# A two-layer hybrid trunk on one core: another first load of x, another order of attention's first products, a later value path in one pair

## The chip, the core and the metric

The kernel runs on one NeuronCore of a Trainium2 chip, as one program. The metric is the device time of one execution in microseconds (us), the median of the runs shown. The profile is of one such execution, taken by the hardware profiler; times in it count from the start of its span.

## The reference

Two layers over 512 tokens of width 2048, batch 1, all in float32. Cut to what matters here:

```python
for l in range(2):
    h = rms_norm(x, norm_g[l])
    proj = h @ w_in[l]                      # 2048 x 6600
    split proj into the inputs of three branches and their gates
    y_ml  = mlstm_branch(...)               # 4 heads of 128
    y_mla = mla_branch(...)                 # 8 heads, low-rank q and kv, rope, causal softmax
    y_rw, v_first = rwkv7_branch(...)       # 8 heads of 64, a recurrence over tokens
    mixed = concat(silu(z) * y for the three)
    x = x + mixed @ w_out[l]
return rms_norm(x, final_norm_g)
# in rwkv7_branch, from layer 1 on:
#   v = v + (v_first - v) * sigmoid(v0 + (v @ v1) @ v2)
# in mla_branch, per head: q from 512, k and v from 256 low-rank columns; q and k have a part with rope
```

## The kernel before

The kernel is written against a tile framework that allocates the buffers, sets the semaphores, and orders each engine's instructions by the program's order and a simulated time line; the order within an engine is then fixed. Each of the matrices is multiplied as three products of a high and a low part (`passes`: hi with xh, hi with xl, lo with xh), so each operand is split first: ScalarE rounds it to the high part (line 150 for weights, 252 for features), VectorE, or GpSimd for attention's weights, subtracts (lines 151, 254, 256).

*The start.* `load_x` reads x, 512 x 2048, in 16 pieces of 256 KB as four tiles `xb` with tokens on the partitions. TensorE transposes them (`feature_major`, line 301), 4 transposes for each of 16 feature tiles, and the result is scaled by `ngc`, the norm's gain, while it is split into `xh` and `xl`. ScalarE sums the squares of the 16 pieces (line 280) for the norm's factor `rb`, which `rstd_cols` spreads by the products `psrs` (line 291). `rb` is applied only to the finished gemm (`normed`, line 542), so the gemm can run before it is known.

*The gemms.* `w_in` is taken in blocks of 256 columns (`ORDER`: `rk0`, `misc`, `rr0`, ... in layer 0), each in four weight tiles `raw` of 512 KB, of which two fit (`Stream`, `wload`, `wsplit`). One block is 96 products of 128 x 512. A block is a generator of eight steps in `bg`; other work calls `bg.step()` or `bg.ensure(name)` and so places the steps in the program. Weights come through SyncE's queue, `nc.sync.dma_start`, with nearly all other loads and stores.

*PSUM.* Eight banks: tag a (`bank`, two), b (`bank2`, two), g (`gbank`, three, for the gemms and attention's up-projections), h (`bank3`, one).

*The recurrence.* `rw_pair(p)` makes the triangular inverse of two heads for eight chunks of 64 tokens, from 16 x 16 blocks up to 32 (`psQ`, `psT`) and 64 (`psQ` again, `psX`), and applies it to two right sides in `AR` (`psW`): one from keys, one, `psR` (line 928), from the values `UV`. In layer 1 the values need gemms `rv0` and `rv1` (line 891) and `psv`, line 893. Each yield lets one gemm step in.

*Attention.* `heads_order` gives the order of generators: `head_in` (products `psqn` and `pskn` of one head), `pair_rope` (`psqr` of two heads and `rope`, VectorE instructions in lines 1234 to 1237), `pair_v` (`psv`, two banks), `head_scores` and `head_out`. The weights are streamed in the same order. While it begins, VectorE also has the end of the gemms (`sg_az`) and the splits `ml` of mixed features left to do.

Of the kernel before, what the change touches and what calls it, by code (L numbers as in the profile page):

```python
# [30 lines left out]
def heads_order():  # L31

    yield from (("rope", 0), ("in", 0), ("v", 0))
    for h in range(8):
        if h < 7:
            yield "in", h + 1
        yield "scores", h
        if h % 2 == 1 and h < 7:
            yield "rope", h // 2 + 1
        yield "out", h  # L40
        if h % 2 == 1 and h < 7:
            yield "v", h // 2 + 1
# [31 lines left out]
def trunk(ctx, tc, a, out):  # L74
# [37 lines left out]
    ngr = x0p.tile([32, 128], F32, name="ngr")  # L112
    dma(ngr, a["norm_g"].rearrange("l (r c) -> (l r) c", c=128))
    xb0 = [x0p.tile([128, D], F32, tag=f"xb{tb}", name=f"xb{tb}_0") for tb in range(4)]

    def load_x(q):

        for tb in range(4):
            dma(xb0[tb][:, q * 512:q * 512 + 512], a["x"][0, tb * 128:(tb + 1) * 128, q * 512:q * 512 + 512])
    load_x(0)  # L120


# [9 lines left out]
    act(warm, eps_rms, AF.Sqrt)  # L132

# [87 lines left out]
    def gemm(l, name, finish, tmajor=False):  # L221

        def run():
            ps = [gbank(f"pg{u}_{name}{l}") for u in range(2)]
# [151 lines left out]
    ngc = const.tile([128, 32], F32, name="ngc")  # L376
    nc.vector.tensor_copy(ngc, ps[:, 0:32])
    onec = ones[:, 0:1][:, :, None]
    ss = sum_squares(x0p, "x0")
# [137 lines left out]
    for l in range(DEPTH):  # L517
# [117 lines left out]
        if l == 0:  # L635
            x_tiles(0)
            for q in range(4):
# [56 lines left out]
        def rw_pair(p, l=l):  # L694
# [194 lines left out]
            v = fetch("rv")  # L889
            if l > 0:  # L890
                bg.ensure("rv1")
                ps = bank(f"psv2_{nm}")
                mm(ps, lhsT=v2[:, p * 128:(p + 1) * 128], rhs=kept["vv"], start=True, stop=True)
                yield
                s = tmp("vs")
                sigm(s, ps, pch(R_V0 + p))
                vf = tmp("vf")
                dma(vf, vf_d[p])
                tt(vf, vf, v, ALU.subtract)
                tt(vf, vf, s, ALU.mult)  # L900
                tt(v, v, vf, ALU.add)
            tt(bv, bv, v, ALU.mult)
            dma(tail_d[p, 0], bv)

            UV = rp.tile([128, 2, 8, 64], F32, tag="UV", name=f"UV{nm}")
            token_major(lambda tb: v[:, tb * 128:(tb + 1) * 128], lambda h: UV[hs[1 - h], h], "v")
# [26 lines left out]
            nc.scalar.copy(AR[:, even, 64:128], psR[0])  # L933
            nc.scalar.copy(AR[hs[0], odd, 64:128], psR[1][hs[1]])
            nc.vector.tensor_copy(AR[hs[1], odd, 64:128], psR[1][hs[0]])
# [17 lines left out]
            for j in (1, 3):  # L953
                nc.scalar.copy(Q[q4[j], odd, :], psQ[1][q4[j ^ 2]])
                nc.vector.tensor_copy(Q[q4[j], even, :], psQ[0][q4[j]])
            yield
            with in_order():
                psX = cross32([(3, 2), (1, 0)], lambda i, c: Q[q4[i], c, :], lambda i, c: X32[q4[i], c, :], "psX64",
                              (bank, bank2), (0, 1))
            for j in (0, 2):  # L960
                nc.scalar.copy(X[q4[j], odd, 32:64], psX[1][q4[j ^ 2]])
                nc.vector.tensor_copy(X[q4[j], even, 32:64], psX[0][q4[j]])
            yield
# [570 lines left out]
_INS = ['x', 'positions', 'norm_g', 'w_in', 'ml_conv_w', 'ml_conv_b', 'ml_i_bias', 'ml_f_bias', 'ml_norm_g',  # L1534
# [21 lines left out]
```

## Time and profile before

| | |
|---|---|
| median of 3 runs | 1965.5 us (1965.09 to 1966.24) |
| the profiled execution | 1964.04 us, its span 1962.3 us |
| TensorE busy | 1932.2 us, 98% |
| VectorE, ScalarE, GpSimd busy | 1245.6, 863.5, 136.4 us |
| mean granted clock of TensorE | 0.997 of full speed |
| read from and written to HBM | 212.45 and 50.35 MB |

The span runs from the first to the last instruction. A busy TensorE is one with a matmul in flight: matmuls are pipelined and overlap, so the sum of their durations is more than the time they take one after the other. The granted clock tells which share of full speed (2.4 GHz) the chip gave TensorE in a stretch; half of it is the lower level, 1.2 GHz.

### The profile page before, as it was taken

To read this page: it belongs to the slowest core of one execution; us is meant where nothing else is said; L and a number is where in the kernel's file an instruction comes from. 1 tells how busy PE (TensorE), PEld (TensorE's weight loads), DVE (VectorE), ACT (ScalarE), POOL (GpSimd) and SP (SyncE) were. 2 spreads that over 40 slices of the span, in tenths; PEclk is the share of its full clock that TensorE was granted. 3 is DMA by queue.
4 is the path that set the end of the run, shared out by engine and by line. 5 is a ranking of instruction groups with operands and counts; after the bars stand their busy time and mean duration, and the time that the engine had idled before them with its cause. 6 is when DMAs were issued, how large, how long until landed. Compare 5 with 4: busy or idle time off the path is not lost. (4 is left out here: it accounts for less than half of the span.)

```text
span 1962.3 us, 31796 instructions
## 1 busy us (share of the span) xinstructions
PE 1932.2 (98%) x12544; PEld 1607.1 (82%) x12544; DVE 1245.6 (63%) x2179; ACT 863.5 (44%) x1509; POOL 136.4 (7%) x168
## 2 busy tenths in 40 slices
PE   8999999999999999999999999999999999999998
PEld 6888888888888878788888788988878888788886
DVE  6876776685766398533366558676847676884343
ACT  6534352434556356422263234433434564563233
POOL 4010010100000031000001001010100000210000
PEclk9999999999999999999999999999999999999999
DMA  5443444335655443334444444344345564343334
GB/s 178 131 141 106 126 127 119 115 110 173 188 167 177 120 119 121 103 136 133 135 111 138 121 122 129 118 131 122 106 125 189 167 209 137 105 133 115 118 121 158
DMA packets 246394, 264.86 MB, mean 135 GB/s; under 512 B 49972, under 2 KB 178174, under 8 KB 246246
## 3 DMA queue, kind: packets, MB, share of 16 engines
q1 hardware_dynamic: 245398, 261.88, 43.8%
q8 instruction: 98, 1.61, 0.3%
q0 software_dynamic: 848, 0.97, 0.2%
q14 instruction: 50, 0.41, 0.1%
HBM read 212.45 MB, written 50.35 MB: 134 GB/s over the span
## 5 line engine op out<-in xcount | busy, mean ns | idle before, releaser
L1405 PE MATMUL po<-whi_o,mh 128*128 128x512 f32 x512 | 200.2, 391 | 0.1
L1405 PE MATMUL po<-whi_o,ml 128*128 128x512 f32 x512 | 199.3, 389 | 0.0
L151 DVE TENSOR_TENSOR wlo_o<-raw_o,whi_o 128x1024 fp32r<-128x1024 f32 x64 | 78.3, 1225 | 188.7 <-ACT whi_o L150 187.6
L1405 PE MATMUL po<-wlo_o,mh 128*128 128x512 f32 x512 | 187.8, 390 | 0.0
L150 ACT ACTIVATE whi_o<-raw_o 128x1024 fp32r<-128x1024 f32 x64 | 67.7, 1059 | 204.7 <-PE po L1405 168.2
L1405 PEld LDWEIGHTS po<-whi_o,mh 128*128 128x128 f32 x512 | 96.1, 188 | 20.1 <-DVE Vl L254 0.6
L1405 PEld LDWEIGHTS po<-wlo_o,mh 128*128 128x128 f32 x512 | 96.0, 188 | 20.0
L1405 PEld LDWEIGHTS po<-whi_o,ml 128*128 128x128 f32 x512 | 96.2, 188 | 19.7
L239 PE MATMUL pg_az<-xl,whi_az 128*128 128x512 f32 x256 | 100.7, 393 | 0.0
L239 PE MATMUL pg_az<-xh,whi_az 128*128 128x512 f32 x256 | 100.6, 393 | 0.0
L239 PE MATMUL pg_az<-xh,wlo_az 128*128 128x512 f32 x256 | 99.5, 394 | 0.0
L235 PE MATMUL pg_mv<-whi_mv,xh 128*128 128x256 f32 x256 | 72.9, 285 | 0.0
L235 PE MATMUL pg_mv<-whi_mv,xl 128*128 128x256 f32 x256 | 72.7, 285 | 0.0
L235 PE MATMUL pg_mv<-wlo_mv,xh 128*128 128x256 f32 x256 | 72.4, 285 | 0.0
L770 POOL TENSOR_TENSOR bk<-kk,Ei 64x512 f32<-64x512 f32 x16 | 26.5, 1657 | 505.2 <-DVE kk L757 176.5
L151 DVE TENSOR_TENSOR wlo_az<-raw_az,whi_az 128x1024 fp32r<-128x1024 f32 x32 | 39.1, 1223 | 31.0 <-ACT whi_az L150 30.8
L239 PEld LDWEIGHTS pg_az<-xh,wlo_az 128*128 128x128 f32 x256 | 48.1, 188 | 9.5
L239 PEld LDWEIGHTS pg_az<-xh,whi_az 128*128 128x128 f32 x256 | 48.1, 188 | 9.4
L239 PEld LDWEIGHTS pg_az<-xl,whi_az 128*128 128x128 f32 x256 | 48.2, 188 | 9.3
L239 PE MATMUL pg_rk<-xh,whi_rk 128*128 128x512 f32 x128 | 50.9, 401 | 1.3 <-ACT xh L252 1.3
L239 PE MATMUL pg_rk<-xl,whi_rk 128*128 128x512 f32 x128 | 51.5, 403 | 0.0
L150 ACT ACTIVATE whi_az<-raw_az 128x1024 fp32r<-128x1024 f32 x32 | 33.7, 1053 | 39.7 <-PE pg_az L239 26.6
(576 smaller groups left out, 5547.7 us busy)
## 6 DMA issues: line engine op xcount, KB each, us to landing
raw_o<-in_w_out_dram SPq DMA_DIRECT2D x64, 512.0 KB
raw_az<-in_w_in_dram SPq DMA_DIRECT2D x32, 512.0 KB
raw_rk<-in_w_in_dram SPq DMA_DIRECT2D x16, 512.0 KB
raw_rr<-in_w_in_dram SPq DMA_DIRECT2D x16, 512.0 KB
raw_rv<-in_w_in_dram SPq DMA_DIRECT2D x16, 512.0 KB
raw_rz<-in_w_in_dram SPq DMA_DIRECT2D x16, 512.0 KB
raw_mq<-in_w_in_dram SPq DMA_DIRECT2D x16, 512.0 KB
raw_mk<-in_w_in_dram SPq DMA_DIRECT2D x16, 512.0 KB
```

Source lines behind the costliest of these rows:

```text
L150: act(hi, raw, AF.Copy)
L151: (nc.gpsimd if name[0] == "u" or name in ("misc0_0", "misc0_1") else nc.vector).tensor_tensor(lo, raw, hi.bitcast(F32), ALU.subtract)
L235: mm(ps[u][:, (tb % 2) * 256:(tb % 2) * 256 + 256], lhsT=xx[:, sl], rhs=w[:, i, :], start=(k == 0 and n == 0 and tb % 2 == 0), stop=(k == ...
L239: mm(ps[u], lhsT=w[:, i, u * 128:(u + 1) * 128], rhs=xx, start=(k == 0 and n == 0), stop=(k == 15 and n == 2))
L770: nc.gpsimd.tensor_tensor(bk[q, :, slot, :], x[q].rearrange(c64, t=64), Ei[q].rearrange(c64, t=64), ALU.mult)
L1405: mm(pss[tb], lhsT=xx[:, sl], rhs=w, start=(k == korder[0] and j == 0), stop=(k == korder[15] and j == 2))
```

## The change

*The start.* The host passes x transposed (`xt`) and the gains transposed (`norm_gt`) as further inputs. The first weight tile is loaded first, then `ngc` directly, then 16 feature tiles `xr` of 256 KB, which are split without a transpose. After them x is loaded once more with tokens on the partitions, in four loads of 1 MB, for four squares. Fourteen products of zeros run on TensorE at the beginning. The `misc` gemm of layer 0 takes banks of tag a instead of g.

*Attention.* The first three entries of the order become in, rope, v.

*Layer 1, pair 0.* Fetching the values, their residual, the transposes to `UV` (now the inner function `values`) and `psR` with its three copies move behind the inverse's second level: `values` ahead of the products `psX`, and `psR` right behind these, in banks a and b.

```diff
-    yield from (("rope", 0), ("in", 0), ("v", 0))
+    yield from (("in", 0), ("rope", 0), ("v", 0))
...
-    ngr = x0p.tile([32, 128], F32, name="ngr")
-    dma(ngr, a["norm_g"].rearrange("l (r c) -> (l r) c", c=128))
-    xb0 = [x0p.tile([128, D], F32, tag=f"xb{tb}", name=f"xb{tb}_0") for tb in range(4)]
+    xr = [x0p.tile([128, T], F32, tag=f"xr{k}", name=f"xr{k}") for k in range(16)]
     def load_x(q):
-        for tb in range(4):
-            dma(xb0[tb][:, q * 512:q * 512 + 512], a["x"][0, tb * 128:(tb + 1) * 128, q * 512:q * 512 + 512])
-    load_x(0)
+        for k in range(4 * q, 4 * q + 4):
+            dma(xr[k], a["xt"][k * 128:(k + 1) * 128, :])
...
+    zero = x0p.tile([128, T], BF16, name="zero")
+    nc.vector.memset(zero, 0.0)
+    ps = bank2("pswarm")
+    for _ in range(14):
+        mm(ps, lhsT=zero[:, 0:128], rhs=zero, start=True, stop=True)
...
-            ps = [gbank(f"pg{u}_{name}{l}") for u in range(2)]
+            ps = [(bank if (l, name) == (0, "misc") else gbank)(f"pg{u}_{name}{l}") for u in range(2)]
...
     ws.ahead(raws=1)
-    load_x(1)
+    ngc = const.tile([128, 32], F32, name="ngc")
+    dma(ngc, a["norm_gt"])
+    load_x(0)
     ws.ahead()
-    load_x(2)
-    load_x(3)
-    ps = bank("psng")
-    nc.tensor.transpose(ps[:, 0:32], ngr, idf[0:32, 0:32])
...
+    for q in range(1, 4):
+        load_x(q)
+    ss = sum_squares(x0p, "x0")
+    xb0 = [x0p.tile([128, D], F32, name=f"xb{tb}_0") for tb in range(4)]
+    for tb in range(4):
+        dma(xb0[tb], a["x"][0, tb * 128:(tb + 1) * 128, :])
...
-                    feature_major(0, k, lambda tb: xb0[tb][:, k * 128:k * 128 + 128], (bank, bank2)[k % 2])
+                    split2(xh[k], xl[k], xr[k], scale=ngc[:, k:k + 1])
...
-            for q in range(4):
-                for tb in range(4):
-                    add_square(x0p, ss[:, tb, q:q + 1], xb0[tb][:, q * 512:q * 512 + 512], f"x0_{tb}_{q}")
+            for tb in range(4):
+                add_square(x0p, ss[:, tb, 0:1], xb0[tb], f"x0_{tb}")
...
+            late = l > 0 and p == 0
...
+            if not late:
+                for _ in values():
+                    yield
...
-                psR = cross(64, lambda h, c: GG[hs[1 - h], h, c, 0:64], lambda h, c: UV[hs[1 - h], h, c, :], "psR",
-                            (bank2, bank2))
+                if not late:
+                    psR = right((bank2, bank2))
...
+            if late:
+                for _ in values():
+                    yield
             yield
             with in_order():
                 psX = cross32([(3, 2), (1, 0)], lambda i, c: Q[q4[i], c, :], lambda i, c: X32[q4[i], c, :], "psX64",
                               (bank, bank2), (0, 1))
+                if late:
+                    psR = right((bank, bank2))
...
+            if late:
+                right_back(psR)
             yield
```

## Rows read from the trace of the kernel before

**Rows 1.** The page's table of engines: busy us, share of the span, instructions.
```profile
PE 1932.2 (98%) x12544; PEld 1607.1 (82%) x12544; DVE 1245.6 (63%) x2179; ACT 863.5 (44%) x1509; POOL 136.4 (7%) x168
```
**Rows 2.** The waits of TensorE: us in total, times, the longest.
```profile
PE psv L1291 <- DVE qrf L1236: 5.0, 2, 2.6
...
PE psTv L779 <- DVE TX L862: 0.6, 1, 0.6
```
**Rows 3.** Stretches of the start: length, busy per engine, granted clock, DMA share, GB/s.
```profile
2.00:10.00 8.00, 4.26 (x17) 3.11 (x17) 2.23 (x11) 4.43 (x12) 6.09 (x17) 1.00 0.88 267
10.00:18.00 8.00, 7.16 (x30) 5.58 (x31) 5.13 (x7) 6.88 (x15) 4.83 (x17) 0.79 1.06 391
12.20:15.60 3.40, 3.40 (x11) 2.48 (x10) 1.75 (x4) 2.30 (x6) 3.04 (x14) 0.51 1.07 398
20.00:24.00 4.00, 4.00 (x23) 3.29 (x22) 2.24 (x7) 3.97 (x10) 0.00 (x0) 1.00 0.04 10
43.40:100.00 56.60, 56.60 (x254) 46.31 (x253) 46.84 (x63) 30.59 (x37) 4.79 (x5) 1.00 0.47 134
```
**Rows 4.** Timeline of SyncE's queue from 7 us on, and ScalarE's last split of `rk0`.
```profile
7.33 6.85 SPq L119 DMA_DIRECT2D xb<-in_x_dram  x8
14.79 0.38 SPq L323 DMA_DIRECT2D raw_rk<-in_w_in_dram  x1
...
23.34 0.40 SPq L323 DMA_DIRECT2D raw_rk<-in_w_in_dram  x1
...
27.12 1.06 ACT L150 ACTIVATE whi_rk<-raw_rk 128x1024 fp32r<-128x1024 f32 x1 [1.43 <-DMA raw_rk<-in_w_in_dram]
```
**Rows 5.** Timeline of TensorE: the first gemm's first products, the second gemm's first.
```profile
11.23 0.47 PE L239 MATMUL pg_rk<-xh,whi_rk 128*128 128x512 f32 x1
11.54 0.39 PE L239 MATMUL pg_rk<-xl,whi_rk 128*128 128x512 f32 x1
11.77 0.40 PE L239 MATMUL pg_rk<-xh,whi_rk 128*128 128x512 f32 x1
...
43.42 0.40 PE L239 MATMUL pg_misc<-xh,whi_misc 128*128 128x512 f32 x1
```
**Rows 6.** Groups by line, 0 to 45 us: busy us, mean ns, idle before.
```profile
L301 PE MATMUL psx<-idf,xb 128*128 128x128 f32 x64 | 11.9, 318 | 3.5 <-DMA xb<-in_x_dram 3.3
L280 ACT ACTIVATE junk_x<-xb 128x512 f32<-128x512 f32 x16 | 10.0, 625 | 3.0 <-DMA xb<-in_x_dram 2.9
L150 ACT ACTIVATE whi_rk<-raw_rk 128x1024 fp32r<-128x1024 f32 x4 | 4.2, 1054 | 2.1 <-DMA raw_rk<-in_w_in_dram 2.1
L132 ACT ACT_TABLE_LOAD x1 | 1.3, 1283 | 0.8 <-PEq L1544 0.8
L291 PE MATMUL psrs<-idf,sg_rw 128*128 128x128 f32 x8 | 1.1, 274 | 0.0
```
**Rows 7.** Stretches where attention begins, layers 0 and 1, and layer 1's pair 0.
```profile
688.00:698.00 10.00, 7.42 (x35) 5.90 (x34) 9.91 (x12) 4.80 (x9) 3.35 (x2) 1.00 0.67 214
698.00:702.00 4.00, 4.00 (x23) 4.00 (x23) 4.00 (x6) 3.10 (x6) 1.82 (x1) 0.57 0.63 193
1673.00:1680.00 7.00, 6.91 (x45) 6.14 (x44) 6.91 (x10) 4.71 (x8) 1.87 (x1) 1.00 0.39 109
1040.00:1180.00 140.00, 140.00 (x945) 110.31 (x944) 80.20 (x118) 47.45 (x69) 7.43 (x5) 1.00 0.41 123
```
**Rows 8.** Timeline of attention's beginning: layer 0, then layer 1.
```profile
694.00 0.68 DVE L1234 TENSOR_TENSOR rt<-psqr,sinn 32x512 f32<-32x512 f32 x1
698.84 1.82 POOL L151 TENSOR_TENSOR wlo_uqk<-raw_uqk,whi_uqk 128x768 fp32r<-128x768 f32 x1 [5.42 <-ACT whi_uqk L150]
702.31 0.40 PE L1263 MATMUL psqn<-cqh,whi_uqk 128*128 128x512 f32 x1
...
1669.02 0.68 DVE L1234 TENSOR_TENSOR rt<-psqr,sinn 32x512 f32<-32x512 f32 x1
1676.19 0.40 PE L1263 MATMUL psqn<-cqh,whi_uqk 128*128 128x512 f32 x1
```

More of the change, by code (lines that the diff above doesn't have):

```diff
@@ L369, in trunk @@
     ws.ahead(raws=1)
-    load_x(1)
+    ngc = const.tile([128, 32], F32, name="ngc")
+    dma(ngc, a["norm_gt"])
+    load_x(0)
     ws.ahead()
-    load_x(2)
-    load_x(3)
-    ps = bank("psng")
-    nc.tensor.transpose(ps[:, 0:32], ngr, idf[0:32, 0:32])
-    ngc = const.tile([128, 32], F32, name="ngc")
-    nc.vector.tensor_copy(ngc, ps[:, 0:32])
+    for q in range(1, 4):
[4 more added lines that the diff above has]
+        dma(xb0[tb], a["x"][0, tb * 128:(tb + 1) * 128, :])
     onec = ones[:, 0:1][:, :, None]
-    ss = sum_squares(x0p, "x0")
     prm, prh, omu, gbias = [], [], [], []
@@ L636, in trunk @@
             x_tiles(0)
+            xh, xl = xT[0]
             for q in range(4):
                 for k in range(4 * q, 4 * q + 4):
-                    feature_major(0, k, lambda tb: xb0[tb][:, k * 128:k * 128 + 128], (bank, bank2)[k % 2])
+                    split2(xh[k], xl[k], xr[k], scale=ngc[:, k:k + 1])
                 if q == 1:
@@ L888, in rw_pair, with values, right, right_back @@
             yield
[L889 to L903, printed above, removed]
-            UV = rp.tile([128, 2, 8, 64], F32, tag="UV", name=f"UV{nm}")
-            token_major(lambda tb: v[:, tb * 128:(tb + 1) * 128], lambda h: UV[hs[1 - h], h], "v")
+            late = l > 0 and p == 0
+            UV = rp.tile([128, 2, 8, 64], F32, tag="UV", name=f"UV{nm}")
+            def values():
+                v = fetch("rv")
+                if l > 0:
+                    bg.ensure("rv1")
+                    ps = bank(f"psv2_{nm}")
+                    mm(ps, lhsT=v2[:, p * 128:(p + 1) * 128], rhs=kept["vv"], start=True, stop=True)
+                    yield
+                    s = tmp("vs")
+                    sigm(s, ps, pch(R_V0 + p))
+                    vf = tmp("vf")
+                    dma(vf, vf_d[p])
+                    tt(vf, vf, v, ALU.subtract)
+                    tt(vf, vf, s, ALU.mult)
+                    tt(v, v, vf, ALU.add)
+                tt(bv, bv, v, ALU.mult)
+                dma(tail_d[p, 0], bv)
+                token_major(lambda tb: v[:, tb * 128:(tb + 1) * 128], lambda h: UV[hs[1 - h], h], "v")
+            def right(banks_):
+                return cross(64, lambda h, c: GG[hs[1 - h], h, c, 0:64], lambda h, c: UV[hs[1 - h], h, c, :], "psR", banks_)
+            def right_back(psR):
+                nc.scalar.copy(AR[:, even, 64:128], psR[0])
+                nc.scalar.copy(AR[hs[0], odd, 64:128], psR[1][hs[1]])
+                nc.vector.tensor_copy(AR[hs[1], odd, 64:128], psR[1][hs[0]])
+            if not late:
+                for _ in values():
+                    yield
             for _ in range(2):
@@ L932, in rw_pair @@
             tt(Q[:, even, :], psQ[0], mqb, ALU.mult)
-            nc.scalar.copy(AR[:, even, 64:128], psR[0])
-            nc.scalar.copy(AR[hs[0], odd, 64:128], psR[1][hs[1]])
-            nc.vector.tensor_copy(AR[hs[1], odd, 64:128], psR[1][hs[0]])
+            if not late:
+                right_back(psR)
             yield
@@ L955, in rw_pair @@
                 nc.vector.tensor_copy(Q[q4[j], even, :], psQ[0][q4[j]])
+            if late:
+                for _ in values():
+                    yield
             yield
@@ L962, in rw_pair @@
                 nc.vector.tensor_copy(X[q4[j], even, 32:64], psX[0][q4[j]])
+            if late:
+                right_back(psR)
             yield
@@ L1530, in trunk @@
     x_ctx.close()
-_INS = ['x', 'positions', 'norm_g', 'w_in', 'ml_conv_w', 'ml_conv_b', 'ml_i_bias', 'ml_f_bias', 'ml_norm_g',
+_INS = ['x', 'positions', 'xt', 'norm_gt', 'w_in', 'ml_conv_w', 'ml_conv_b', 'ml_i_bias', 'ml_f_bias', 'ml_norm_g',
         'mla_q_norm_g', 'mla_w_uq', 'mla_kv_norm_g', 'mla_w_ukv', 'rw_mu', 'rw_w0', 'rw_w2', 'rw_a0', 'rw_a2',
@@ L1545 @@
     arrays, args = {}, {}
+    inputs["xt"] = np.asarray(inputs["x"])[0].T
+    inputs["norm_gt"] = np.asarray(inputs["norm_g"]).reshape(-1, 128).T
     for name in _INS:
```

## The prediction

> **What bounds the kernel now.** I read the page's table of engines first: TensorE is busy for 1932.2 of 1962.3 us [rows 1]. Work taken off another engine gains nothing by itself; the change can win or lose only where TensorE waits, runs at the lower clock, or does work that can go, and all its idle time together is 30.1 us. The view of TensorE's waits says where that idle time lies as far as it has a releaser: above all two waits of products `psv` for VectorE, 5.0 us in all, the longer 2.6 [rows 2]. Most of the rest is the start and the end. At the start the first real product begins at 11.23, and the second gemm (`misc`) at 43.42 [rows 5]. From 43.4 to 100 us TensorE is busy for 56.60 of 56.60 [rows 3], so 43.42 is the mark against which the start is measured: what moves it moves the end.
>
> **The change at the start.** It has two sides.
>
> What goes: 64 transposes `psx`, 11.9 us of overlapped busy time [rows 6]. The first gemm has 96 products 0.23 us apart [rows 5], 21.9 us of work, and took 32.2 us from 11.23 to 43.42. If data were there, TensorE could begin at about 7 us (half a MB of weights and a quarter MB of x at 267 GB/s from 2 us on [rows 3], the landing, the splits) and be through at about 31.
>
> What comes: x is loaded a second time, by four loads of 1 MB, and in the program these stand behind the features and ahead of the third weight tile, which can't be asked for before the first one is split, since there are two raw buffers. SyncE issues in the order of the program: in the trace the last pieces of x, then the third weight tile at 14.79, then 15 small parameter loads, then the fourth at 23.34 [rows 4]. All go into one queue. Up to the third tile it held 16 x 0.262 + 3 x 0.524 = 5.77 MB. From 2 to 18 us, 267 x 8 + 391 x 8 = 5.26 MB came; the last 0.51 at 391 GB/s end at 19.3, and from 20 us on the rate is 10 [rows 3]: the tile landed last in line. With 4.19 MB more in front of it, at 391, it lands 10.7 us later, at 30.0. A page of the Trainium skill, "DMA: Bandwidth & Descriptors" (section Measured), has 425 GB/s for its largest transfer. By that figure the extra x takes an estimated 9.9 us and the sum is 0.8 us less; no transfer here has rows as long as the new loads'.
>
> TensorE then does 48 of the 96 products early, by about 19, and stands until the third tile is split. ScalarE does that in 1.05 us [rows 6]. In the program the squares of the four x blocks come ahead of it. A square of 512 columns takes 0.625 us and a copy of 1024 takes 1.054 [rows 6], so a square of 2048 is about 1.9, and 2.1 with the read-out of its sum, an estimate from these two. The last block lands 1.3 us before the weights (0.524 MB at 391), at 28.7, is squared by 30.8, and the split ends at 31.9. With the split first it is 31.1; with the norm's square root and its table load (1.3 [rows 6], and 0.4 for the rest, an estimate) ahead as well, 33.6. I take 31.9, since both earlier things are ready earlier.
>
> From there: 48 products at 0.23 are 10.9 us. The clock: after the sparse start 3.4 us had a granted clock of 0.51, the 1.2 GHz level [rows 3]; that costs 3.4 x 0.5 = 1.7 us. I take it again after a hole of some 12 us, although the 14 warming products have been run: these help only the 48 products that must wait anyhow. The granted clock was also 0.57 from 698 to 702, behind a wait of 2.6 us, and 1.00 from 1673 to 1680, behind one of 2.4 [rows 2, 7]; this hole is longer than both. The Trainium skill's page "TensorE: Matmul & The Clock Gate" (section HAM oscillation) has an array that waits for DMA fall back to half rate, which speaks against warming it ahead of such a wait. By that rule the sum stays; were the clock kept, it is 1.7 us less.
>
> The 8 products `psrs` (1.1 us as busy time [rows 6]), the parameters' transposes and one small one stay, about 1.2 us together, behind the hole, as what they need lands late too. Sum: 31.9 + 10.9 + 1.7 + 1.2 = 45.7 against 43.42: **+2.3 us**. Bounds: 31.1 + 10.9 + 1.2 = 43.2, so -0.2; and 33.6 + 13.8 = 47.4, so +4.0. The fourth tile is what is late next: issued at about 14.79 + 10.7 + 8.55 = 34.0, split from 3.8 us after its issue (27.12 against 23.34 [rows 4]), so by 38.9, and wanted at 31.9 + 5.5 + 1.7 = 39.1. It is just covered; each us more costs one.
>
> The other edits here cost nothing on that path: `ngc` comes by a 16 KB load instead of a transpose, `misc` takes PSUM banks that nobody else asks for before it ends, and four squares stand for 16.
>
> **Attention's first products.** Before, the order is rope, in, v. There are three gemm banks, so the first `psv` takes the bank of `psqr`, which VectorE empties by five rope instructions of 0.68 us. They begin at 694.0, at the end of a backlog (VectorE is busy for 9.91 of 10 us), so TensorE stands 2.6 us and then runs at 0.57 [rows 2, 7, 8]. Layer 1 has the same with 2.4 us. After, `psv` takes the bank of `psqn`, which is free after one ScalarE and one VectorE instruction. I leave VectorE's backlog as it is: from 694.0 it then does the low parts of q and k (1.4) and then the rope (3.4). `psv` can start at 694.7, before TensorE arrives at 695.1 (702.31 less its own products, the slow clock and the wait). Its 24 products of half width (2.8) end at 697.9; now the next head's `psqn` takes the bank of `psqr`, free at 698.8, and wants low weights that GpSimd had ready at 700.7 [rows 8]. It began at 702.31 before, so 1.6 to 3.5 us are won. In layer 1: 1669.0 + 1.4 + 3.4 = 1673.8 against 1676.19 [rows 8], 2.4 us. Part is given back, for VectorE has no room (4.00 of 4.00 us [rows 7]) and the first scores wait for its rope parts. I take 1.5 per layer, about half of what the rows would allow: **-3.0 us**. Bounds: both waits and the slow stretch whole (2.6 + 2.4 + 4 x 0.43 = 6.7), -6.7; and 0, if the wait only moves to the next `psqn` or the scores.
>
> **Layer 1's first right sides.** The inverse of pair 0 no longer waits for gemm rv1. From 1040 to 1180 us, where that pair lies, TensorE is busy for 140.00 of 140 us [rows 7]: the wait is filled with gemm, and the same products come in another order. The 32 products `psR` and the three copies behind them move ahead of `psW`; the gemm that is left covers them, and without it they are about a microsecond. Cost 0. What it shifts is where the later pairs fall against the gemms, bounded by a wait such as that of `psTv`, 0.6 [rows 2], either way.
>
> **Sum.** The profiled execution took 1964.0 (span 1962.3). 1964.0 + 2.3 - 3.0 + 0 = 1963.3; the median shown is 1.5 above that execution, so **1964.8**. About 0.2% (3.9 us) is what a measurement of this kernel can tell from no change; this is inside it.
>
> **The rivals.**
> 1. The start pays in full: the third weight tile is issued ahead of the second copy of x. For it: x comes 4 us sooner and 64 transposes are gone. Against: the loads kept the program's order up to here [rows 4]. Then `misc` begins at 7 + 21.9 + 1.2 + 1 = 31, 12.3 sooner: 1964.8 - 2.3 - 12.3 = 1950.2.
> 2. Slower: the second copy runs at 267 GB/s, the rate of the first 8 us, instead of 391. Then 4.19 MB take 15.7, all behind the hole is 5.0 later, and the time is 1969.8. It decides against the change (+3.9) below 270 GB/s or so. For it: nothing shows the rate of such loads; against: from 10 us on it was up and stayed.
> 3. The hole is as long, but the split goes first and the clock holds (-0.2), and attention gives 5: 1965.5 - 5.2 = 1960.3.
> 4. Attention does not do what it says, the wait moves whole: 1967.8, inside my own case.
>
> **Chances.** The forecast, with 1961.6 to 1969.4 as its own range, 0.46; rival 1 0.18; rival 2 and what else makes the start late 0.17; rival 3 0.19, of which a little falls short of 0.2%. So faster by over 0.2% 0.35, within 0.2% 0.48, slower 0.17. The range 1951 to 1970.5 holds the forecast, rival 3, half of rival 1 and most of rival 2.
>
> **What would show it.** TensorE idle for about 12 us between 19 and 32, released by ScalarE's split of the third `rk` tile; half clock behind it; `misc` beginning near 46. At 690 to 705 no wait of `psv` for the rope, but one of a microsecond before the next `psqn`. Nothing idle at layer 1's first pair, before or after. The prediction is wrong if the third tile is issued ahead of the four large loads, if these take much less or more than 10.7 us, or if TensorE stands elsewhere for what has been moved.

## The result, and the profile after

The changed kernel takes 1976.61 us (median of 4 runs, 1976.29 to 1977.52) against 1965.87 (1965.09 to 1967.93) for the kernel before, measured beside it: a ratio of 1.0056 [1.0043, 1.0068]. It is slower by about 10.7 us, and outside the predicted range. The profiled execution took 1976.29, its span is 1974.6, 12.3 us more than that of before.

The page's table of engines of the changed kernel, which answers to [rows 1]:

```profile
PE 1930.9 (98%) x12493; PEld 1603.2 (81%) x12493; DVE 1240.1 (63%) x2179; ACT 860.1 (44%) x1485; POOL 139.7 (7%) x168
```

TensorE is busy 1.3 us less than before and idle 13.6 us more. Its waits, by line and releaser (us in total, times, longest), say where, as [rows 2] did:

```profile
PE ps_prm L410 <- DMA gbias<-in_ml_f_bias_dram: 15.0, 1, 15.0
PE psqn L1290 <- DVE qrf L1263: 5.0, 2, 4.1
PE psv L1318 <- DVE qrf L1263: 2.1, 2, 1.1
...
PE psT L940 <- issue: 1.2, 1, 1.2
...
PE pg_rk L243 <- DVE wlo_rk L155: 0.9, 1, 0.9
```

The first is one hole of 15 us, and its releaser is not the third weight tile but small loads behind it. The profile puts it down to the last of them, `gbias`; by the program the transposes need the thirteen that go to `pt`. The second is where the wait for the rope has gone, which the new attention order was to shrink: before it stood at `psv` [rows 2]. TensorE's time line at the start (start, duration, line, tile, count, idle before and releaser), to be read against [rows 5]:

```profile
18.05 0.39 PE L243 MATMUL pg_rk<-xh,wlo_rk 128*128 128x512 f32 x1
33.48 0.89 PE L410 MATMUL ps_prm<-idf,pt 128*128 128x128 f32 x2 [15.04 <-DMA gbias<-in_ml_f_bias_dram]
34.02 0.77 PE L243 MATMUL pg_rk<-xh,whi_rk 128*128 128x512 f32 x1
...
36.94 0.80 PE L243 MATMUL pg_rk<-xh,wlo_rk 128*128 128x512 f32 x1 [0.86 <-DVE wlo_rk L155]
...
40.94 0.86 PE L243 MATMUL pg_rk<-xh,wlo_rk 128*128 128x512 f32 x2
41.65 0.40 PE L243 MATMUL pg_rk<-xh,whi_rk 128*128 128x512 f32 x1
...
43.73 0.39 PE L243 MATMUL pg_rk<-xh,whi_rk 128*128 128x512 f32 x1
43.96 1.05 PE L295 MATMUL psrs<-idf,sg_rw 128*128 128x128 f32 x8
```

After 48 products TensorE stands from 18.4 to 33.5. The two transposes of the parameters come next in its order, ahead of the third tile's products. Behind them products start 0.43 us apart up to 41.65 and 0.23 after: half clock for nearly 8 us. The products of the fourth weight tile begin at 43.73. SyncE's time line, against [rows 4], shows what they waited for:

```profile
13.43 2.43 SPq L384 DMA_DIRECT2D xb<-in_x_dram  x4
16.39 0.38 SPq L327 DMA_DIRECT2D raw_rk<-in_w_in_dram  x1
17.19 0.34 SPq L404 DMA_DIRECT2D pt<-in_ml_conv_b_dram  x1
...
18.34 0.25 SPq L404 DMA_DIRECT2D pt<-in_mla_q_norm_g_dram  x1
20.76 0.23 SPq L404 DMA_DIRECT2D pt<-in_mla_kv_norm_g_dram  x1
23.23 0.31 SPq L404 DMA_DIRECT2D pt<-in_rw_mu_dram  x1
25.63 0.25 SPq L404 DMA_DIRECT2D pt<-in_rw_w_dram  x1
28.08 0.25 SPq L404 DMA_DIRECT2D pt<-in_rw_a_dram  x1
...
31.01 0.31 SPq L407 DMA_DIRECT2D pt<-in_rw_r_k_dram  x1
...
32.11 0.40 SPq L327 DMA_DIRECT2D raw_rk<-in_w_in_dram  x1
```

From 18.3 to 28.1 a small load goes out only every 2.4 us, and each such moment is one at which a block of `xb` lands: ScalarE's squares wait for the four blocks and begin at 20.83, 23.29, 25.70 and 28.14. Two of them, and the splits of the third and the fourth weight tile, in ScalarE's time line:

```profile
20.83 1.91 ACT L284 ACTIVATE junk_x<-xb 128x2048 f32<-128x2048 f32 x1 [1.68 <-DMA xb<-in_x_dram]
23.29 1.91 ACT L284 ACTIVATE junk_x<-xb 128x2048 f32<-128x2048 f32 x1 [0.47 <-DMA xb<-in_x_dram]
...
30.05 1.04 ACT L154 ACTIVATE whi_rk<-raw_rk 128x1024 fp32r<-128x1024 f32 x1
...
37.03 1.06 ACT L154 ACTIVATE whi_rk<-raw_rk 128x1024 fp32r<-128x1024 f32 x1 [5.75 <-DMA raw_rk<-in_w_in_dram]
```

The third tile was split from 30.05 on. TensorE could not use it before 33.5, because an instruction ahead in its queue wanted something else. VectorE's time line shows the same there:

```profile
33.97 0.29 DVE L412 COPY prm<-ps_prm 128x128 f32<-128x128 f32 x1 [3.60 <-PE ps_prm L410]
...
35.70 1.18 DVE L155 TENSOR_TENSOR wlo_rk<-raw_rk,whi_rk 128x1024 fp32r<-128x1024 f32 x1
...
38.12 1.23 DVE L155 TENSOR_TENSOR wlo_rk<-raw_rk,whi_rk 128x1024 fp32r<-128x1024 f32 x1 [1.15 <-ACT whi_rk L154]
```

The copies of the parameters out of `ps_prm` stand ahead of the low part of the third tile, which so is made only at 35.70; that is the 0.86 us for which TensorE waits once more, at 36.94. The fourth tile, last in SyncE's order, went out at 32.11; both its parts were there at 39.4, over 4 us before its first product.

How the delay runs on: first starts of some tiles (of the two in layer 1 the last start), in us, from the line of each tile in the trace, with the two parts alone (s1: the start alone, s2: the attention order alone).

| start of | before | after | s1 | s2 |
|---|---|---|---|---|
| gemm `misc`, layer 0 | 43.4 | 50.4 | 50.5 | 43.7 |
| gemm `rz` | 115.3 | 122.3 | 122.4 | 115.7 |
| gemm `mq` | 217.1 | 225.6 | 227.6 | 217.5 |
| gemm `az` | 588.3 | 597.3 | 599.8 | 588.4 |
| `po`, layer 0 | 791.8 | 800.0 | 803.6 | 791.5 |
| last `az`, layer 1 | 1661.6 | 1671.0 | 1674.7 | 1661.2 |
| last `po`, layer 1 | 1953.1 | 1965.8 | 1967.5 | 1956.8 |

Of 12.7 us at the end, 7.0 are lost before `misc`, 1.5 between `rz` and `mq`, and 3.3 in layer 1's attention; in layer 0's attention 0.8 are won.

### The profile page after: what moved, and what is told of

The parts are those of the page before. It is cut to its first block, busy times and chain, and to the rows that moved or that the text cites. A ratio compares the mean times of both kernels' runs of the same rounds, so it can differ in the third digit from the quotient of the medians.

```text
span 1974.6 us, 31684 instructions
## 1 busy us (share of the span) xinstructions
PE 1930.9 (98%) x12493; PEld 1603.2 (81%) x12493; DVE 1240.1 (63%) x2179; ACT 860.1 (44%) x1485; POOL 139.7 (7%) x168
## 5 line engine op out<-in xcount | busy, mean ns | idle before, releaser
L155 POOL TENSOR_TENSOR wlo_uqk<-raw_uqk,whi_uqk 128x768 fp32r<-128x768 f32 x16 | 29.7, 1858 | 593.9 <-ACT whi_uqk L154 590.7
```

Source lines behind the costliest of these rows:

```text
L155: (nc.gpsimd if name[0] == "u" or name in ("misc0_0", "misc0_1") else nc.vector).tensor_tensor(lo, raw, hi.bitcast(F32), ALU.subtract)
```

## The experiments

Each ratio is to the kernel before, run beside it. s4 to s7, s9, s15 and s16 are edits of the changed kernel, so they also have its attention order, which alone costs 2.3 us (s2).

### The parts alone: s1, s2, s3

**s1_start** is before with the start of the change alone, all of it (the features, the second load, the zeros, the banks for `misc`). Its core:

```
-                    feature_major(0, k, lambda tb: xb0[tb][:, k * 128:k * 128 + 128], (bank, bank2)[k % 2])
+                    split2(xh[k], xl[k], xr[k], scale=ngc[:, k:k + 1])
...
+    for tb in range(4):
+        dma(xb0[tb], a["x"][0, tb * 128:(tb + 1) * 128, :])
```

> The kernel before with the start alone changed (features first, second copy of x, warming products, other banks for misc). Theory 1: nearly all of the start's loss is TensorE standing before the two parameter transposes, which it meets ahead of the third weight tile's products and whose small loads are queued behind the 4 MB of x; so the same hole of about 15 us from 18.4 to 33.5, half clock until about 41.6, misc beginning near 50.4 instead of 43.4, and +7.0 to +8.5 us in all: 1973 to 1974.5 against 1965.9. Rival (the prediction's own step, the hole ends with the third tile, and what is worse in the changed kernel comes from the mixture of edits): misc near 46, about 1968.

1976.67 us, 1.0054 [1.0041, 1.0067]. The start alone costs as much as the whole change: the wait at `ps_prm` is 15.2 us and `misc` begins at 50.5.

**s2_order** is before with the order alone:

```
-    yield from (("rope", 0), ("in", 0), ("v", 0))
+    yield from (("in", 0), ("rope", 0), ("v", 0))
```

> The kernel before with the new order of attention's first products alone. Theory 1: the wait for the rope goes over to the next psqn and in layer 1 grows to about 4 us, since VectorE has two splits of mixed rows ahead of the rope in its order, and these wait for loads that wait for a buffer; layer 0 gains about 1, layer 1 loses about 3: +2 us, 1968 (1966.5 to 1969). Rival (the prediction's term): -3, 1963.

1967.95 us, 1.0014 [1.0006, 1.0023]: a loss of 1.2 to 4.5 us in place of the predicted gain. TensorE's waits, and VectorE's time line where layer 1's attention begins:

```profile
PE psqn L1263 <- DVE qrf L1236: 4.7, 2, 3.8
```

```profile
1667.39 0.67 DVE L254 TENSOR_TENSOR ml<-mr,mh 128x512 fp32r<-128x512 f32 x1
...
1671.23 1.34 DVE L254 TENSOR_TENSOR ml<-mr,mh 128x512 fp32r<-128x512 f32 x2 [2.55 <-ACT mh L252]
1672.59 0.68 DVE L1234 TENSOR_TENSOR rt<-psqr,sinn 32x512 f32<-32x512 f32 x1
```

Two splits of mixed rows stand ahead of the rope in VectorE's order. Their row was asked for at 1668.10, when the split at 1667.39 had given back one of three buffers `mr`; it landed at 1670.57, ScalarE's part came behind it, and VectorE stood for 2.55 us with the rope's operand ready. TensorE's next `psqn`, and windows behind it (stretch, its length and busy time of PE, PEld, DVE, ACT, POOL with counts, granted clock, DMA share, GB/s):

```profile
1676.22 0.77 PE L1263 MATMUL psqn<-cqh,whi_uqk 128*128 128x512 f32 x1 [3.78 <-DVE qrf L1236]
```

```profile
1676.00:1680.00 4.00, 3.78 (x9) 3.04 (x10) 4.00 (x5) 0.81 (x2) 1.70 (x1) 0.50 0.45 115
1680.00:1684.00 4.00, 4.00 (x14) 3.14 (x14) 2.11 (x4) 2.05 (x5) 0.00 (x0) 0.71 0.01 2
```

So this `psqn` begins when it did before (1676.19 [rows 8]): what the order had won is gone. The loss comes behind it: a granted clock of 0.50 and 0.71 in place of 1.00 is 3.2 us of work in these 8, and the next `psv` waits 1.07 us for the second rope.

**s3_late** is before with the late right sides alone, as in the change's diff:

```
+            late = l > 0 and p == 0
...
-                psR = cross(64, lambda h, c: GG[hs[1 - h], h, c, 0:64], lambda h, c: UV[hs[1 - h], h, c, :], "psR",
-                            (bank2, bank2))
+                if not late:
+                    psR = right((bank2, bank2))
...
+                if late:
+                    psR = right((bank, bank2))
```

> The kernel before with layer 1's first right sides made with the last product of the inverse, alone. Theory 1: TensorE has gemm to do either way, so 0 to +1.2 us, 1966 to 1967. Rival (the prediction's term): exactly nothing, 1965.9 within 0.6; a gain of more than 1 us would speak against both.

1965.52 us, 0.9996 [0.9988, 1.0005]: nothing.

### What in the start costs: s4, s5, s6, s7, s9, s15, s16

**s4_defer** asks for the second copy only behind the fourth weight tile:

```
-    for tb in range(4):
-        dma(xb0[tb], a["x"][0, tb * 128:(tb + 1) * 128, :])
...
+            for tb in range(4):
+                dma(xb0[tb], a["x"][0, tb * 128:(tb + 1) * 128, :])
```

> The changed kernel, with the four 1 MB loads of x issued behind the fourth weight tile instead of ahead of the third. Theory 1: the third tile is early and the hole shrinks, but the parameters' loads are still issued only from about 14 us on, and TensorE meets their transposes at about 17; it stands some 5 us there, until 22 or so; misc begins at 36 to 38, 12 to 14 us sooner than in the changed kernel: 1963 to 1965. Rival (the hole belongs to the third weight tile alone): no stand at all before misc, which begins near 31; 19 us sooner, 1957.

1974.15 us, 1.0041 [1.0028, 1.0055]. The hole shrank (`ps_prm` waits 4.2 us) and `misc` began at 40.1, but now the 4.19 MB lie ahead of the weights of `misc`, whose products stood twice for ScalarE's part, 3.1 us together, once for GpSimd's low part (1.8) and once for VectorE's (0.8), and the norm was late. So 10.3 us won at `misc` are 2.5 in the time. The transfer costs ahead of the third tile, and also behind the fourth.

**s5_nocopy** has no second copy and squares the 16 feature tiles instead. Its sums run over the tokens, not over the features, so it doesn't compute the norm; it only shows what the copy costs:

```
-    for tb in range(4):
-        dma(xb0[tb], a["x"][0, tb * 128:(tb + 1) * 128, :])
...
-            for tb in range(4):
-                add_square(x0p, ss[:, tb, 0:1], xb0[tb], f"x0_{tb}")
+            for k in range(16):
+                add_square(x0p, ss[:, k % 4, k // 4:k // 4 + 1], xr[k], f"x0_{k}")
```

> The changed kernel without the second copy of x; the squares for the norm are taken from the feature tiles instead, so the norm's sums are other sums (16 squares of 512 columns). Theory 1 (the 4 MB are what is too much, in two places: ahead of the third tile and the parameters, and, once moved, ahead of the misc weights): TensorE still stands some 4 us before the parameter transposes, until about 22.5, but finds the misc weights there; misc begins at 36 to 38 and runs without a stop: 1962 to 1964. Rival (the misc weights are late by themselves, by their small pieces and GpSimd's splits): the stops of 6 us inside misc stay, 1969.

1968.74 us, 1.0012 [1.0003, 1.0021], 7.9 below the changed kernel. `misc` begins at 40.2 and does not stop; `ps_prm` still waits 3.6 us, and 2.6 us go at the third tile's low part, which VectorE again makes behind the copies out of `ps_prm`. So the copy is the larger part, and the small loads cost also without it. The time is the rival's, but by another way: the lead of 3.2 us at `misc` is 0.8 at layer 0's `az`, and from layer 1's `az` to its last weight tile of `po`, with the changed kernel's attention order, 3.4 are lost.

**s6_packed** keeps the copy where it was and packs the parameters on the host, one load and one for the gate biases per layer:

```
-                for r, s in srcs:
-                    n = s.shape[0] // 128
-                    pdma(pt[r:r + n, :], s.rearrange("(r c) -> r c", c=128))
...
+                pdma(pt, a["prm"][l])
```

> The changed kernel with each layer's parameters packed on the host into one 128 x 128 array, so that one load and one for the gate biases stand where 15 stood; x's second copy stays where it is. Theory 1 (SyncE gets a new load out only as an older one lands, so the 15 small loads take until 32 and hold both the transposes and the fourth tile): the hole ends with the third tile at about 31.5 instead of 33.5, no wait for the fourth tile; misc near 47.5: 1973.5. Rival (the small loads cost nothing beside the 4 MB): 1976.6, as the changed kernel.

1971.16 us, 1.0026 [1.0015, 1.0037], 5.4 below the changed kernel, where 3.1 were expected: 13 small loads fewer. `ps_prm` begins at 29.18 after 10.4 us, the third tile's products at 30.67, `misc` at 45.1.

**s7_pieces** packs them too, and loads the copy in 16 pieces of 256 KB behind the fourth tile, into the buffers of the features.

```
+                for q in range(4):
+                    xb = x0p.tile([128, T], F32, tag=f"xr{4 * tb + q}", name=f"xb{tb}_{q}")
+                    dma(xb, a["x"][0, tb * 128:(tb + 1) * 128, q * 512:q * 512 + 512])
+                    add_square(x0p, ss[:, tb, q:q + 1], xb, f"x0_{tb}_{q}")
```

> The packed parameters, and x's second copy in 16 pieces of 256 KB that are loaded into the buffers of the features, behind the fourth weight tile, with 16 squares. Theory 1: both causes gone; TensorE stands 2 to 4 us around 17 to 21 for the third tile (5.8 MB have to come first at some 390 GB/s), misc begins at 32 to 34, without stops: about 17 us sooner than the changed kernel, 1959 (1957 to 1962). Rival (something else in the start is slow, or the misc weights are late again): 1965 or more.

1967.85 us, 1.0014 [1.0005, 1.0023]. `misc` begins at 36.2, but TensorE stands 7.7 us about it: for the weights of `misc` (3.2 for ScalarE's part, 2.2 for GpSimd's) and for the norm (`psrs`, 2.3). The lead at the mark is given back behind it.

**s9_prmlate** was meant to put the transposes behind the third tile's products, but left TensorE's order as it was, since at that point of the program only 36 of the 96 products stand ahead of them; in the trace they still come behind the 48th.

```
-                nc.tensor.transpose(ps[:, 0:128], pt, idf)
+                tc.keep_in_program_order(nc.tensor.transpose(ps[:, 0:128], pt, idf))
```

> The changed kernel with the two parameter transposes pinned behind the third weight tile's products in TensorE's order; all loads stand where they were. Theory 1 (the transposes wait for the last of 15 small loads, 2.4 us after the third tile is there): the hole ends when the third tile is split, at 31.1 instead of 33.5, but the fourth tile, whose load is still issued at about 32 behind the small ones, is now waited for by about 3 us; so no more than 0 to 2 us are won: 1974.5 to 1976.6. Rival (the place of the transposes is the whole difference between prediction and result): as the packed parameters, 1971.

1976.46 us, 1.0054 [1.0041, 1.0068], `ps_prm` waits 14.8 and `misc` begins at 50.6: it says nothing on the place of the transposes. But its fourth tile went out at 31.12, ahead of the two loads of the gate biases, so the place of these two loads changes nothing.

**s16_prmlate2** does it: three more steps of the gemm come first in the program, and the transposes are issued behind the last of these products, the 72nd. The two loads of the gate biases come later with them, so that the fourth tile goes out ahead of these two, as in s9.

```
-                nc.tensor.transpose(ps[:, 0:128], pt, idf)
+                third = next(i for i in reversed(nc.cur_bb.bb.instructions) if i.engine == mybir.EngineType.PE)
+                with tc.issue_after(third):
+                    nc.tensor.transpose(ps[:, 0:128], pt, idf)
...
+            for _ in range(3):
+                bg.step()
```

> The changed kernel with the two parameter transposes really behind the third tile's products in TensorE's order (three more steps of the gemm are traced ahead of them); the loads stand as they were. Theory 1 (small loads late, and the fourth tile's load behind them): the hole ends at 31.1 with the third tile, 2.4 us sooner, and the wait for the fourth tile grows; 1974 to 1976. Rival (only the place of the transposes was wrong in the prediction): as the packed parameters, 1971.

1973.28 us, 1.0044 [1.0029, 1.0060], 3.3 below the changed kernel; its profiled span is 5.2 shorter. TensorE's time line and windows:

```profile
30.72 0.80 PE L243 MATMUL pg_rk<-xh,whi_rk 128*128 128x512 f32 x1 [12.36 <-ACT whi_rk L154]
...
35.58 0.45 PE L243 MATMUL pg_rk<-xh,whi_rk 128*128 128x512 f32 x1
```

```profile
34.00:36.00 2.00, 2.00 (x7) 1.57 (x6) 0.00 (x0) 0.87 (x1) 0.00 (x0) 0.58 0.99 289
36.00:38.00 2.00, 2.00 (x11) 1.61 (x10) 1.78 (x3) 0.19 (x1) 0.49 (x2) 1.00 0.57 75
```

The hole is now released by the split, as the prediction had it: 12.4 us, half clock until 35.6, no wait for a low part, the fourth tile in time as in the changed kernel, `misc` at 45.6. In this execution the loads ran some 0.4 us earlier, which is part of the 4.8 won at `misc`. The time falls between the two theories and its interval holds both, so the step is read from the trace and not from the time.

**s15_nowarm** is the changed kernel without its 14 products of zeros.

```
-    for _ in range(14):
-        mm(ps, lhsT=zero[:, 0:128], rhs=zero, start=True, stop=True)
```

> The changed kernel without the 14 warming products. Theory 1 and the prediction alike: the first 48 products wait for the third tile anyhow, so nothing: 1976.6 within 1. Rival (the warming products matter, or cost something, in the first 18 us): 1.7 us or more either way.

1975.41 us, 1.0051 [1.0037, 1.0065]: they are worth nothing here. The 1.2 us less lie inside the intervals.

### Attention: s8, s10, s12

**s8_inv** is before with a third order, in, v, rope.

```
-    yield from (("rope", 0), ("in", 0), ("v", 0))
+    yield from (("in", 0), ("v", 0), ("rope", 0))
```

> The kernel before with attention's first products in the order in, v, rope. Theory 1 (the waits of TensorE there come from who takes over the rope's bank, and VectorE empties it late): the bank is now taken over only by head 1's products, both waits of 2.4 and 2.6 us and the slow clock behind the first go, and only a part comes back before the scores: -3 to -5, about 1962. Rival (VectorE's backlog sets the first scores anyway, the wait moves there): 1965.6, as before.

1968.03 us, 1.0008 [0.9999, 1.0017]. No gain: `psv` still waits for the rope, 3.4 us at the longest. That putting the rope last would clear the way was wrong.

**s10_ropefix** (new order) and **s12_oldrope** (old order) are before with the splits of mixed rows issued behind the first rope:

```
+            if hp == 0:
+                att["rope"] = next(i for i in reversed(nc.cur_bb.bb.instructions) if i.engine == mybir.EngineType.DVE)
...
-            split2(mh[k], ml[k], t)
+            with tc.issue_after(att["rope"]):
+                split2(mh[k], ml[k], t)
```

> The kernel before with the new order of attention's first products, and with the splits of the mixed rows (ScalarE and VectorE parts traced in mixed_in) issued behind the first pair's rope on VectorE. Theory 1 (the 3.8 us wait in layer 1 is VectorE standing 2.5 us for a mixed row whose load waits for a buffer, with the rope behind it): the wait falls to about 1 us or less in both layers, 3 to 5 us less than the new order alone: 1963 to 1965. Rival (VectorE has no room, what is put back comes before the scores): 1968, as the new order alone.

1969.17 us, 1.0017 [1.0008, 1.0025]: no better than s2. Layer 1's first wait went, 3.8 us at `psqn` for the rope became 0.2 for GpSimd's low weights, so the splits were its cause. But the splits put off are then done ahead of the second rope. TensorE's waits in both layers show it at the `psv` of the next two heads:

```profile
717.74 0.38 PE L1293 MATMUL psv<-whi_uv,ckh 128*128 128x256 f32 x1 [3.09 <-DVE qrf L1236]
...
1694.17 0.39 PE L1293 MATMUL psv<-whi_uv,ckh 128*128 128x256 f32 x1 [2.90 <-DVE qrf L1236]
```

In s2 these two waits were 1.07 each. The wait moved by one pair of heads, and the half clock with it: 0.60 from 717.7 to 722, 0.59 from 1694 to 1698.

> The kernel before, its order of attention kept, with the splits of the mixed rows issued behind the first pair's rope on VectorE. Theory 1: psqr is done about 2.5 us before VectorE comes to the rope, so both waits of psv (2.6 and 2.4) shrink to under 1, and the slow clock behind the first goes: -3 to -5, 1961 to 1963. Rival (VectorE has no room): 1965.9.

1963.53 us, 0.9985 [0.9976, 0.9994]: in the old order the same edit gains 2.9 us, 1.2 to 4.7. The waits for the rope fall from 5.0 to 1.0; of 3.0 that come in their place, 2.7 lie in layer 1, at the second bank of `psv`. The two profiled executions are of one length (spans 1962.2 and 1962.3): 2.1 won at layer 0's `po` are lost again by the end of layer 1, so the gain rests on the times of all runs and its place isn't shown.

### What the start can give: s11, s13, s14

**s11_start** has the start and the late right sides, the old attention order, parameters packed and transposed on the host (no `ps_prm`), the copy behind the fourth tile, and gemm `rr0` ahead of `misc`.

```
-ORDER = [["rk0", "misc", "rr0", "rv0", "rz0", "rk1", "rr1", "rv1"] + _REST,
+ORDER = [["rk0", "rr0", "misc", "rv0", "rz0", "rk1", "rr1", "rv1"] + _REST,
...
+            with tc.issue_after(fourth):
+                xb0 = [x0p.tile([128, 4, T], F32, tag=f"xq{tb}", name=f"xb{tb}_0").rearrange("p a f -> p (a f)") for tb in range(4)]
```

> A version meant to beat both kernels: the changed start and the late right sides with the old order of attention; parameters packed and transposed on the host (no transposes on TensorE), x's second copy loaded into the feature buffers behind the fourth weight tile, and gemm rr0 ahead of misc. Theory 1 (each of the start's losses is a load that stands in line behind something that is wanted later): no stop over 2 us, gemm two begins at 32 to 34 and the three first gemms end near 77 instead of 87; -8 to -11 against the kernel before: 1955 to 1958. Rival (what the start gains is given back in the first pair, whose inputs come from misc and are not earlier): 1962 to 1966.

1966.67 us, 1.0003 [0.9993, 1.0012]. The second gemm begins at 35.0 and `mq` at 207.6, 9.5 us sooner than before; at `az` 4.2 of these are left, and layer 0's `po` begins 1.9 later. Of the 5.3 lost between `mq` and `az`, two waits in the recurrence show 3.5 (2.0 at `psTk`, and a stop of 1.5, last section); where the rest goes isn't shown.

**s13_ceiling** is s11 with the old `ORDER` and, as s5, without the copy, so it doesn't compute the norm either:

```
-ORDER = [["rk0", "rr0", "misc", "rv0", "rz0", "rk1", "rr1", "rv1"] + _REST,
+ORDER = [["rk0", "misc", "rr0", "rv0", "rz0", "rk1", "rr1", "rv1"] + _REST,
...
+            for k in range(16):
+                add_square(x0p, ss[:, k % 4, k // 4:k // 4 + 1], xr[k], f"x0_{k}")
```

> The ceiling of the start: the kernel before with the changed start and the late right sides (old order of attention), without the second copy of x (squares of the feature tiles, so other sums in the norm), and with the parameters packed and transposed on the host, two loads a layer and no transposes on TensorE. Theory 1 (the start's loss is the copy and the small loads, nothing else): TensorE waits some 2 us for the third tile near 18 to 20, misc begins at 33 to 35; -4 to -8 against the kernel before: 1958 to 1962. Rival (what is won at the start comes back as waits in later stages): 1965 to 1966.

1960.75 us, 0.9976 [0.9967, 0.9984]: `misc` at 36.9, a gain of 4.7 us [3.1, 6.5].

**s14_onesq** is s13 with the reference's norm, still without a copy: the squares of the features are summed over the partitions by 16 products with a matrix of ones. It also has the edit of s12.

```
+                act(sq, xr[k], AF.Square)
+                mm(psq, lhsT=onesr, rhs=sq, start=(k == 0), stop=(k == 15))
+            rb = const.tile([128, T], F32, tag="rb", name="rb0")
+            rsqrt(rb, psq, 1.0 / D, eps_rms)
```

> A version meant to beat both kernels: as the ceiling, but with the right norm: the squares of the feature tiles are added up over the partitions by 16 products with ones on TensorE, which leave the sums on every partition; and the splits of the mixed rows behind the rope, old order of attention. Theory 1: the ceiling's time, less 2 for the attention, plus about 3 for the 16 products: -5 to -8 against the kernel before: 1958 to 1961. Rival: only the rope's 2 us are left, 1963.5.

1961.83 us, 0.9975 [0.9965, 0.9986]: faster than both kernels, by 4.9 us [2.8, 6.9] than before and by some 15 than the changed one. Its TensorE stands hardly at all at the start; the time line there:

```profile
20.68 0.50 PE L633 MATMUL psrs<-sq,onesr 128*128 128x512 f32 x1 [0.84 <-ACT sq L632]
22.23 0.50 PE L243 MATMUL pg_rk<-xh,whi_rk 128*128 128x512 f32 x1 [1.06 <-ACT whi_rk L154]
22.57 0.40 PE L243 MATMUL pg_rk<-xl,whi_rk 128*128 128x512 f32 x1
22.81 0.39 PE L243 MATMUL pg_rk<-xh,whi_rk 128*128 128x512 f32 x1
```

Stops of 0.84 and 1.06 us in place of 15, products 0.23 apart behind them (the full clock), `misc` at 34.6. Of this lead of 8.8 us 6.7 are left at layer 0's `po` (785.1) and 2.2 at the last `po` (1950.9): layer 1 gives most of it back. So it is no better than s13 within the intervals, though its start is shorter and it has the edit of s12.

## Why the prediction was wrong, and where it was right

**The start: +2.3 predicted, +7.0 at `misc`, some 11 us in all.** Most of the chain held. The third tile was predicted to land at 30.0 and its split to end at 31.9; the split began at 30.05, right behind the last square and without a wait for the tile, and ended at 31.1. A square of 2048 columns took 1.91, as estimated. The windows of the changed kernel, with the columns as above, give the rate and the clock:

```profile
18.00:26.00 8.00, 0.44 (x2) 0.02 (x1) 3.46 (x11) 5.46 (x7) 1.69 (x3) 0.69 1.01 425
...
33.00:41.00 8.00, 6.66 (x16) 4.66 (x17) 4.97 (x13) 1.58 (x2) 2.52 (x7) 0.50 0.72 184
...
50.40:100.00 49.60, 49.60 (x223) 40.51 (x223) 37.65 (x50) 29.18 (x36) 2.78 (x3) 1.00 0.40 116
```

The copy came at 425 GB/s, against 391 assumed. The Trainium skill's figure for its largest transfer (page "DMA: Bandwidth & Descriptors", section Measured) is the same 425. The clock was 0.50 behind the hole. From `misc` on TensorE was busy without a gap, so for a loss the mark was right: 7.0 at `misc` are still there at `az`. A lead at it is partly given back (s7, s11, s14).

The step that failed is this: "The 8 products `psrs` (1.1 us as busy time [rows 6]), the parameters' transposes and one small one stay, about 1.2 us together, behind the hole, as what they need lands late too." The transposes stood at the hole's end, ahead of the third tile's products, and what they need landed later than that tile. The prediction gave the fifteen small loads 8.55 us between the third tile and the fourth, but let them hold up nothing else; SyncE let them out one by one as the large blocks landed, and the last that the transposes need went out at 31.01. In place of 31.9 + 10.9 + 1.7 + 1.2 = 45.7 came 34.0 (first product) + 10.9 + 3.4 (half clock: 6.8 us of work between 34.02 and 41.65) + 0.9 (the third tile's low part, behind the parameters' copies on VectorE) + 1.2 = 50.4. The fourth tile, "just covered" in the prediction, cost nothing: it went out 1.9 us sooner than the 34.0 forecast. s16 shows that this is the step: with the transposes behind the products, and the loads in the order of s9, where `misc` began at 50.6, the stand ends with the split, the wait for the low part is gone, and `misc` begins at 45.6, 4.8 us sooner than in the changed kernel. That this is the predicted 45.7 is in part luck: there the hole ended 1.2 us sooner than predicted, and the half clock cost 0.7 more.

The half clock alone was mis-sized too: 1.7 predicted, 3.4 here, 2.4 in s16 (30.72 to 35.58 at half). The Trainium skill's page "TensorE: Matmul & The Clock Gate" (section HAM oscillation) has an array that waits for DMA restart at half rate; the granted 0.50 agrees, and s15 shows that the warming ahead of such a wait gave nothing.

Between `misc` and `mq` s1 loses 3.4 us more, which the prediction didn't have. Its time line, in pair 0:

```profile
146.97 0.72 PE L925 MATMUL psT<-Qa,X 32*32 32x32 f32 x61
149.32 0.25 PE L925 MATMUL psT<-Qa,X 32*32 32x32 f32 x3 [1.63 <-issue]
```

A stop of 1.63 us, then a granted clock of 0.83 from 150 to 160, 1.7 us: together 3.3. In the changed kernel the stop is 1.25 and the clock stays at 1.00; that is the 1.5 of the table. Before has no stop there. What the traces say of its cause stands in the last section.

**Attention: -3.0 predicted, +2.3 alone.** The mechanism was half right. `psv`'s waits for the rope went, and in layer 0 the wait before the next `psqn` was the microsecond foreseen (0.87). In layer 1 it was 4.1. The step that failed is "I leave VectorE's backlog as it is". The new order let VectorE come to splits of mixed rows whose data were not there. Before, it was busy throughout there:

```profile
1666.00:1674.00 8.00, 4.87 (x26) 3.92 (x26) 7.92 (x10) 3.19 (x5) 4.25 (x3) 1.00 0.75 232
```

VectorE's, SyncE's and ScalarE's time lines of the changed kernel:

```profile
1677.14 0.69 DVE L258 TENSOR_TENSOR ml<-mr,mh 128x512 fp32r<-128x512 f32 x1
...
1681.33 1.41 DVE L258 TENSOR_TENSOR ml<-mr,mh 128x512 fp32r<-128x512 f32 x2 [2.49 <-ACT mh L256]
1682.75 0.68 DVE L1261 TENSOR_TENSOR rt<-psqr,sinn 32x512 f32<-32x512 f32 x1
```

```profile
1677.86 0.32 SPq L1423 DMA_DIRECT2D mr<-mix_d  x1
```

```profile
1680.66 1.35 ACT L256 ACTIVATE mh<-mr 128x512 fp32r<-128x512 f32 x2 [2.55 <-DMA mr<-mix_d]
```

The chain is split, buffer, load, split, rope: 2.8 us from the load's issue to its use, 2.5 of them idle on VectorE. The prediction also gave the moved wait no half clock; 3.2 us of it followed in s2, and the granted clock was 0.58 from 1686 to 1690 in the changed kernel. s10 shows that the splits cause this wait, and also that removing it doesn't make the order pay: it comes back at the next rope. What would make the new order pay was not found.

**Layer 1's right sides: 0 predicted, 0 measured** (s3, -0.1% to +0.05%).

**The rivals.** Rival 2 had the right sign and the wrong mechanism: the rate was higher than assumed, not lower. Rival 1's condition, the third tile ahead of the copy, was made in s4, s7 and s11; its price of 14.6 us was too large, since the 4 MB stand in the way of the next weights (s4, s7), and a lead in the gemms is partly given back later (s11). Even with no copy and the small loads packed, the start and the late right sides give 4.7 (s13).

The parts alone sum to 11.0 + 2.3 - 0.1 = 13.2 against 10.7; about 1.8 of the difference would be the shorter stop in pair 0, which s1's profiled execution has in full. s1's five runs spread from 1973.7 to 1978.0, so the difference isn't clear of noise.

## What to carry to other kernels

When a load or a stall is moved, follow not only the data that the next product needs but whatever stands ahead of that product in its engine's own order, and what that in turn waits for: here two transposes of parameters, in front of a tile that was ready, turned a cost of 2 us into 7. Many small loads behind large ones are not free; pack them or put them where nobody waits. Before loading a tensor a second time in another layout, look whether the sum it is for can be made from what is there: 16 products with ones took the place of 4 MB, and the kernel that had them, with packed parameters and the old order of attention, was 4.9 us faster than before.

## What was not expected of the hardware

SyncE held small loads back behind large ones. With 1 MB blocks on the way it issued one per landing, 2.4 us apart (20.76, 23.23, 25.63, 28.08). By the count of issues, four blocks, a weight tile and three small loads were under way when it stopped at 18.3, eight in all. With 256 KB pieces ahead, in s4, the same small loads went out about 0.7 us apart (14.11 to 18.20).

TensorE stopped for 1.1 to 1.6 us near the end of 64 products `psT` of 32 x 32 (after 61 in the changed kernel, earlier in s11), with nothing that the profile shows to wait for ("issue"). It did so in the changed kernel and in most kernels with its start (s1, s4, s5, s6, s9 and s16 in pair 0, s11 at 447.8 us; s13 stopped 1.7 us right behind these products), not in before or in before with one of the other edits (s2, s3, s8, s10, s12), and not in s7, s14 and s15. No run was made on its cause, but the traces point at the loading of TensorE's own instructions. The changed kernel's page has, among its DMA queues:

```profile
q8 instruction: 98, 1.61, 0.3%
```

These are 98 loads of 16 KB, and 98 times 256 is just the 25 088 products and weight loads of the kernel before [rows 1]. In pair 0 every stop comes behind 1473 or 1474 of TensorE's records; in s11 it comes behind 6594, which is 20 x 256 more than 1474. In all nine traces a load of q8 began 0.6 us or less before the first of the 64 products (in s13 0.04 behind it), and 2.2 to 2.5 us before TensorE went on. In s7, s14 and s15 that load began 2.0 to 2.1 us before them. So the stop is probably a wait for instructions that were asked for too late for such short products. What made the load late, and whether moving it would end the stop, was not tried.
